# Routed experts: half of the gate weights' row blocks as plain float32, w1 and w3 side by side, no low halves on GpSimd, one path for all block sizes

## The chip, the cores and the metric

The kernel runs on one core of a Trainium2 chip, in one launch. The metric is the device time of one execution in microseconds. A time that is given here is that of the profiled execution, or the median of runs where it says so.

## What is computed

A token sequence of 512 rows and 1024 columns goes through two layers of a hybrid mixer (first_block), then through a layer with differential attention, retention and a mixture of experts. The change lies in the mixture's routed experts alone:

```
_, top_e = lax.top_k(jnp.where(emask, sel, -jnp.inf), TOP_K)      # 8 of 64 experts for each token
...
xb = h_pad[tok]
yb = (jax.nn.silu(xb @ w1[e]) * (xb @ w3[e])) @ w2[e]
return acc.at[tok].add((yb * wt[:, None].astype(yb.dtype)).astype(acc.dtype)), None
```

w1 and w3, the gate weights, are 1024 x 256, w2 is 256 x 1024, all float32: 3 MB for an expert, 64 experts.

## The kernel before

Every operation goes through a recorder (`Rec`, line 411 issues them all, so that the profile shows one line for everything). A planner (`plan`, `attempt`) sorts the recorded operations for each engine by its own costs; the order of the program is its result, and each engine then works in that order. Tiles come from pools: `s2` has 70 half tiles of 128x512 (named b in the profile), `ad` has four whole tiles of 128x1024 (named raw), `wr` three more.

The expert stage (`moe`, line 2280) runs the 64 experts in a fixed order of slots: experts 0 to 3 in the first four, the others sorted by their load when it is known. Each slot has a capacity (`CAPS`: 192, 128, 96, 80, 64, 48 or 32 rows). A slot of 192 is worked in two blocks, of 128 and 64 rows, so there are 68 blocks: 35 of more than 64 rows and 33 of up to 64. A loop behind them takes what did not fit; it is a few instructions if nothing is left.

For an expert:

- `w_raws` (line 2158) loads the weights on the SP queue: twelve half tiles of 128x512, the first two as one whole tile from `ad` (`RAWN`), in the order w1, w3, w2. A load is held back until an earlier expert has reached a certain point (`hold`, `RAHEAD`).
- `w_load` (line 2180) splits each half tile into a high and a low half: ScalarE copies it to the rounded type float32r (hi), and a subtraction raw - hi gives lo. The subtraction is VectorE's (DVE), but for the half tiles 2, 5, 8 and 11 it is GpSimd's (POOL):

```
nc.scalar.activation(hi, raw, AF.Copy)
sub = nc.gpsimd if 4 * i + q in POOL_LO else nc.vector
sub.tensor_tensor(out=lo, in0=raw, in1=hi.bitcast(F32), op=OP.subtract)
```

- `block` (line 2203) makes the list of tokens, gathers their rows X with an indirect DMA of POOL (raw<-h2d), transposes X on TensorE (PE) in two halves of four column blocks, and splits each half into hi and lo.
- `ffn` (line 2109) is the gate pass, the activation and the second product. For a block of more than 64 rows each of 8 column blocks takes three rounded matmuls (hi·hi, hi·lo, lo·hi) for w1 and three for w3, each with 256 moving columns: 48. For a smaller block of c rows hi and lo of X stand side by side as 2c stationary columns, and each column block takes two matmuls for w1 and two for w3: 32; the two parts are then transposed and added (the fold). The second product takes 12 rounded matmuls with 512 columns.
- Y, scaled by the token's weight (two multiplications on DVE, raw<-ps,m,b), stands in a whole tile of the pool `ad` and is added to the result in DRAM by an indirect DMA of POOL (accd<-raw), the scatter.

Of the kernel before, what the change touches and what calls it, by code (L numbers as in the profile page):

```python
# [12 lines left out]
F32 = mybir.dt.float32  # L13
# [21 lines left out]
POOL_LO = (2, 5, 8, 11)  # L35
# [13 lines left out]
FOLD = "v"  # L49
# [93 lines left out]
def layout2(a, o):  # L143
# [20 lines left out]
    for n in ("exp_w1", "exp_w3", "exp_w2"):  # L164
        o[n] = a[n + "_2"][0]
# [1695 lines left out]
class K3(K2):  # L1861
# [247 lines left out]
    def ffn(self, w13, w2, xs, c=128):  # L2109
        nc = self.nc  # L2110
        ph = self.psum("mm")
        for i in range(2):
            self.seen.setdefault(3 * self.turn + i, len(nc.ops))
            po = slice(256 * i, 256 * i + 256)
            if c > 64:
                self.mm3(ph[:c, po], [(xs[k], w13[i][k]) for k in range(8)])
                continue
            for k in range(8):
                for n, w in enumerate(w13[i][k]):
                    nc.tensor.matmul(ph[:2 * c, po], xs[k], w, start=(k + n == 0), stop=(k + n == 8))  # L2120
        th, ac, ha = (self.t2() for _ in range(3))
        pt = self.psum("tr")
        if c > 64:
            th, ac, ha = th[:c, :256], ac[:c, :256], ha[:c, :256]
            a, b = ph[:c, 0:256], ph[:c, 256:512]
        else:
            both, s = self.t2()[:2 * c], self.t2()[:, :4 * c]
            nc.scalar.activation(both, ph[:2 * c], AF.Copy)
            for q in range(4):
                self.tr(pt[:, 2 * c * q:2 * c * q + 2 * c], both[:, 128 * q:128 * q + 128])  # L2130
            parts = pt[:, :8 * c].rearrange("p (q h c) -> p q h c", q=4, h=2)
            s3 = s.rearrange("p (q c) -> p q c", q=4)
            if FOLD == "r":
                nc.vector.tensor_reduce(s3, parts.rearrange("p q h c -> p q c h"), axis=AX.X, op=OP.add)
            else:
                nc.scalar.activation(s3, parts[:, :, 1, :], AF.Copy)
                (nc.vector if FOLD == "v" else nc.gpsimd).tensor_tensor(out=s3, in0=s3, in1=parts[:, :, 0, :], op=OP.add)
            th, ac, ha = th[:, :2 * c], ac[:, :2 * c], ha[:, :2 * c]
            a, b = s[:, :2 * c], s[:, 2 * c:4 * c]
# [3 lines left out]
        if c > 64:  # L2143
            for j in range(2):
                self.tr(pt[:, c * j:c * j + c], ha[:, 128 * j:128 * j + 128])
            ha = pt[:, :2 * c]
        hh, hl = self.t2(F32R, tag="wh")[:, :2 * c], self.t2(F32R, tag="wl")[:, :2 * c]
        nc.scalar.activation(hh, ha, AF.Copy, scale=0.5)
        nc.vector.scalar_tensor_tensor(hl, ha, 0.5, hh.bitcast(F32), op0=OP.mult, op1=OP.subtract)
# [8 lines left out]
    def w_raws(self, es):  # L2158
        nc, A = self.nc, self.A
        for at, e in enumerate(es):  # L2160
            for i, n in enumerate(("exp_w1", "exp_w3", "exp_w2")):
                for h in range(2):
                    big = 2 * i + h in RAWN[min(at, len(RAWN) - 1)]
                    for cs in (slice(0, 1024),) if big else (slice(0, 512), slice(512, 1024)):
                        nc.bias = -STEP * (at + 1)
                        self.hold(3 * at + i - RAHEAD)
                        if i == h == cs.start == 0 and not isinstance(e, int):
                            e = nc.call("sync", *e)
                        f = lambda a, h=h, i=i, cs=cs: (a.rearrange("(h p k) f -> p h (k f)", h=2, k=4) if i < 2 else
                                                        a.rearrange("(j p) d -> p j d", j=2))[:, h, cs]  # L2170
                        raw = self.t2(tag="ad" if big else "s2")
                        if isinstance(e, int):
# [215 lines left out]
```

## Time and profile before

| | us |
|---|---|
| three runs | 2492.75, 2490.65, 2480.94 |
| median | 2490.65 |
| span of the profiled execution (its own time; none is listed apart from it) | 2496.7 |
| PE busy | 2153.1 (86%) |
| DVE busy | 1899.5 (76%) |
| ScalarE busy | 1244.2 (50%) |
| POOL busy | 909.6 (36%) |

The profile is of one execution. Busy times are unions of an engine's instructions over the whole span, so they mix stages with different limits; a stage is read from the slices and from a table by stretches. The last chain of the profile holds only the final few microseconds, and tells nothing of the stage. The expert stage begins at about 1600 us and ends at about 2475 us.

### The profile page before, as it was taken

Reading aid. Unit: us, or ns where it says so; the run is one execution under the profiler, and the core shown is the slowest. Engines: PE = TensorE matmul, PEld = TensorE weight load, DVE = VectorE, ACT = ScalarE, POOL = GpSimd, SP = SyncE. Lnnn points to the kernel's source line nnn. Section 1 sums busy time; section 2 is a strip of 40 time slices with the busy share of each in tenths; the row PEclk is TensorE's granted clock in tenths of the full one; section 3 lists DMA queues with packets and bytes.
Section 4 is the critical chain, followed back from the end, with each engine's and each line's share of the span. In section 5 each row is a group of like instructions: output and inputs, shape, how many; then the busy total and the mean of one; then the engine's idle time right before and its main releaser. Section 6 shows DMA issues by size and latency. Waiting matters only on the chain. (4 is left out here: it accounts for less than half of the span.)

```text
span 2496.7 us, 36786 instructions
## 1 busy us (share of the span) xinstructions
PE 2153.1 (86%) x11824; PEld 1740.9 (70%) x11824; DVE 1899.5 (76%) x3679; ACT 1244.2 (50%) x2594; POOL 909.6 (36%) x649
## 2 busy tenths in 40 slices
PE   6889988999999999999987898778878887777774
PEld 4678865677879877778865686677767766556553
DVE  7994568765885467778426766899999989999996
ACT  6554456443542554544323543455555556566664
POOL 3363334000130000010001221565666777767764
PEclk9998999999999999999989799889999988878987
DMA  5334354223331322241111253688988998888983
GB/s 183 114 104 146 110 167 153 71 64 133 97 96 43 127 80 73 63 158 67 59 43 34 68 194 132 184 262 256 292 260 245 287 276 273 263 267 281 294 259 108
DMA packets 191206, 398.40 MB, mean 160 GB/s; under 512 B 32169, under 2 KB 48297, under 8 KB 191010
## 3 DMA queue, kind: packets, MB, share of 16 engines
q1 hardware_dynamic: 178050, 356.24, 43.2%
q0 software_dynamic: 12960, 39.79, 7.5%
q8 instruction: 93, 1.52, 0.3%
q14 instruction: 103, 0.84, 0.1%
HBM read 358.44 MB, written 41.63 MB: 160 GB/s over the span
## 5 line engine op out<-in xcount | busy, mean ns | idle before, releaser
L411 PE MATMUL ps<-b,b 128*128 128x512 f32 (+11 forms) x9700 | 1956.0, 360 | 187.7 <-DVE b L411 126.5
L411 PEld LDWEIGHTS ps<-b,b 128*128 128x128 f32 (+3 forms) x9700 | 1532.1, 188 | 529.7 <-DVE b L411 156.0
L411 DVE TENSOR_TENSOR b<-b,b 128x512 fp32r<-128x512 f32 (+11 forms) x656 | 574.5, 900 | 34.5 <-ACT b L411 16.7
L411 ACT ACTIVATE b<-b 128x512 fp32r<-128x512 f32 (+6 forms) x896 | 481.3, 594 | 196.3 <-DVE b L411 152.9
L411 ACT ACTIVATE b<-ps 128x512 f32<-128x512 f32 (+13 forms) x661 | 279.1, 445 | 560.3 <-PE ps L411 498.9
L411 DVE TENSOR_TENSOR b<-raw,b 128x512 fp32r<-128x512 f32 (+2 forms) x468 | 379.7, 826 | 186.1 <-ACT b L411 171.6
L411 POOL TENSOR_TENSOR b<-b,b 128x512 fp32r<-128x512 f32 (+2 forms) x318 | 442.6, 1447 | 207.3 <-DVE b L411 99.2
L411 ACT ACTIVATE b<-raw 128x512 fp32r<-128x512 f32 (+3 forms) x476 | 284.7, 614 | 342.5 <-PE ps L411 247.7
L411 PE MATMUL ps<-const,b 128*128 128x128 f32 (+3 forms) x964 | 172.4, 299 | 90.1 <-DVE b L411 71.5
L411 PEld LDWEIGHTS ps<-const,b 128*128 128x128 f32 (+3 forms) x964 | 125.3, 157 | 125.8 <-DVE b L411 80.2
L411 POOL TENSOR_TENSOR raw<-raw,raw 128x1024 f32<-128x1024 f32 x56 | 139.8, 2504 | 156.9 <-ACT raw L411 128.0
L411 POOL TENSOR_TENSOR m<-m,mhalf 128x1 f32<-128x1 f32 (+2 forms) x54 | 53.6, 994 | 302.8 <-DVE m L411 298.5
L411 POOL DMA_INDIRECT raw<-h2d,m x68 | 101.8, 1498 | 167.0 <-DVE m L411 87.2
L411 POOL MEMSET b<- 64x512 f32 (+4 forms) x19 | 8.4, 453 | 399.2 <-PE ps L411 324.6
L411 POOL DMA_INDIRECT accd<-raw,m x72 | 125.2, 1739 | 62.6 <-DVE raw L411 24.3
L411 DVE TENSOR_TENSOR b<-ps,b 128x512 fp32r<-128x512 f32 (+8 forms) x204 | 101.3, 513 | 25.4 <-ACT b L411 16.3
L411 DVE TENSOR_TENSOR b<-b,ps 128x512 f32<-128x512 f32 (+5 forms) x150 | 80.5, 545 | 48.3 <-PE ps L411 46.8
L411 DVE TENSOR_REDUCE m<-ps 128x1 f32<-128x256 f32 (+9 forms) x196 | 74.9, 392 | 41.8 <-PE ps L411 39.9
L411 DVE SCALAR_TENSOR_TENSOR raw<-ps,m,b 96x512 f32<-96x512 f32 (+5 forms) x136 | 95.7, 735 | 6.8 <-PE ps L411 6.8
L411 DVE SCALAR_TENSOR_TENSOR b<-b,b 128x512 f32<-128x512 f32 (+4 forms) x124 | 83.8, 677 | 16.1 <-ACT b L411 11.7
L411 DVE SCALAR_TENSOR_TENSOR b<-ps,cols,b 128x511 f32<-128x511 f32 (+3 forms) x118 | 86.8, 742 | 7.6 <-ACT b L411 6.6
L411 PE MATMUL ps<-const,raw 64*128 64x64 f32 (+5 forms) x544 | 63.5, 257 | 30.6 <-DVE b L411 17.4
(137 smaller groups left out, 1129.4 us busy)
## 6 DMA issues: line engine op xcount, KB each, us to landing
b<-in_exp_w_dram SPq DMA_DIRECT2D x640, 256.0 KB
raw<-in_wi_dram SPq DMA_DIRECT2D x100, 512.0 KB
raw<-in_exp_w_dram SPq DMA_DIRECT2D x64, 512.0 KB
raw<-in_adaw_dram SPq DMA_DIRECT2D x48, 512.0 KB
raw<-in_wo_dram SPq DMA_DIRECT2D x40, 512.0 KB
raw<-in_wuq_dram SPq DMA_DIRECT2D x24, 192.0 KB
b<-in_x_dram SPq DMA_DIRECT2D x16, 256.0 KB
zd<-b SPq DMA_DIRECT2D x16, 256.0 KB
```

Source lines behind the costliest of these rows:

```text
L411: getattr(getattr(nc, o.eng), o.fn)(*[real(x) for x in o.a], **{m: real(x) for m, x in o.k.items()})
```

## The change

The weights of an expert come in one array `ew`: four tiles of 128x1024 for w1 and w3, then two for w2. In a tile of the first four the half tiles are two row blocks k, each with w1's 256 columns and w3's 256 beside each other, so that one matmul with 512 moving columns serves both. Row blocks 0 to 3 (`NATIVE = 4`) are used as they were loaded, with X copied and not split, by one float32 matmul each; row blocks 4 to 7 and w2 are split as before, always with the subtraction on DVE, and take three rounded matmuls each. The path for blocks of up to 64 rows is gone. The whole tile (`RAWN`) now holds row blocks 0 and 1.

```diff
-POOL_LO = (2, 5, 8, 11)
+NATIVE = 4
...
-    for n in ("exp_w1", "exp_w3", "exp_w2"):
-        o[n] = a[n + "_2"][0]
+    w13 = np.stack([a[n + "_2"][0].reshape(64, 2, 128, 2, 2, 256) for n in ("exp_w1", "exp_w3")], axis=5)
+    w2 = a["exp_w2_2"][0].reshape(64, 2, 128, 1024)
+    o["ew"] = np.concatenate([w13.transpose(0, 1, 3, 2, 4, 5, 6).reshape(64, 4, 128, 1024), w2], axis=1)
...
     def ffn(self, w13, w2, xs, c=128):
...
-            if c > 64:
-                self.mm3(ph[:c, po], [(xs[k], w13[i][k]) for k in range(8)])
+        for k in range(8):
...
+            if k < NATIVE:
+                nc.tensor.matmul(ph, xs[k], w13[k], start=(k == 0), stop=(k == 7))
                 continue
-            for k in range(8):
-                for n, w in enumerate(w13[i][k]):
-                    nc.tensor.matmul(ph[:2 * c, po], xs[k], w, start=(k + n == 0), stop=(k + n == 8))
+            (xh, xl), (wh, wl) = xs[k], w13[k]
+            for n, (x, w) in enumerate(((xh, wh), (xl, wh), (xh, wl))):
+                nc.tensor.matmul(ph, x, w, start=(k + n == 0), stop=(k + n == 9))
...
     def w_load(self, at):
...
+            if q < NATIVE:
+                W.append(self.raw[p])
+                continue
...
-                nc.scalar.activation(hi, raw, AF.Copy)
-                sub = nc.gpsimd if 4 * i + q in POOL_LO else nc.vector
-                sub.tensor_tensor(out=lo, in0=raw, in1=hi.bitcast(F32), op=OP.subtract)
+            self.split(self.raw[p], hi, lo)
...
     def block(self, w, pos, aux, c=128):
...
-            if c > 64:
-                hi, lo = self.t2(F32R, tag="wh")[:, :4 * c], self.t2(F32R, tag="wl")[:, :4 * c]
-                self.split(px, hi, lo)
-                xs += [(hi[:, c * k:c * k + c], lo[:, c * k:c * k + c]) for k in range(4)]
+            if h < NATIVE // 4:
+                x = self.t2(tag="wh")[:, :4 * c]
+                nc.scalar.activation(x, px, AF.Copy)
+                xs += [x[:, c * k:c * k + c] for k in range(4)]
                 continue
```

The planner sorts the changed program anew, so the order on every engine is another one from the expert stage on. Three places follow.

POOL in the middle of the stage, before (a gather is raw<-h2d, a scatter accd<-raw; the others are low halves, b<-raw weights and their hi):

```order
L411 DMA raw_150<-h2d,m_17_93 80x1024
L411 TENSOR_TENSOR b_18769<-b_18387,b_18753 128x512
L411 TENSOR_TENSOR b_18802<-b_18434,b_18783 128x512
L411 TENSOR_TENSOR b_18817<-b_18440,b_18806 128x512
L411 DMA accd<-raw_145,m_3_79 640x1024
L411 TENSOR_TENSOR b_18868<-b_18470,b_18843 128x512
L411 DMA raw_151<-h2d,m_50_126 80x1024
L411 TENSOR_TENSOR b_18950<-b_18589,b_18932 128x512
L411 TENSOR_TENSOR b_18963<-b_18593,b_18953 128x512
L411 TENSOR_TENSOR b_18985<-b_18577,b_18973 128x512
L411 TENSOR_TENSOR b_19030<-b_18659,b_19018 128x512
L411 DMA accd<-raw_146,m_1_77 640x1024
```

and now:

```order
L411 DMA raw_150<-h2d,m_28_104 48x1024
L411 DMA accd<-raw_148,m_47_123 640x1024
L411 DMA raw_151<-h2d,m_10_86 48x1024
L411 DMA accd<-raw_145,m_29_105 640x1024
L411 DMA accd<-raw_145,m_8_84 640x1024
L411 DMA raw_149<-h2d,m_9_85 48x1024
L411 DMA raw_150<-h2d,m_5_81 48x1024
```

Between a gather and a scatter nothing is left on POOL.

PE at the head of the gate pass of a block of 64 rows, before (ps is the sum, then X's tile of hi and lo beside each other is the second name, a half of a weight's half tile the first):

```order
L411 MATMUL ps_68<-b_20081,b_20231 128x256
L411 MATMUL ps_68<-b_20106,b_20231 128x256
...
L411 MATMUL ps_68<-b_20114,b_20231 128x256
L411 MATMUL ps_68<-b_20139,b_20231 128x256
...
L411 MATMUL ps_68<-b_20097,b_20239 128x256
L411 MATMUL ps_68<-b_20116,b_20239 128x256
```

and now (raw_147, b_17447 and b_17450 are raw weights, x2 are two in a row):

```order
L411 MATMUL ps_66<-raw_147,b_17815 64x512 x2
L411 MATMUL ps_66<-b_17447,b_17815 64x512
L411 MATMUL ps_66<-b_17450,b_17815 64x512
L411 MATMUL ps_66<-b_17723,b_17828 64x512
L411 MATMUL ps_66<-b_17723,b_17837 64x512
L411 MATMUL ps_66<-b_17738,b_17828 64x512
L411 MATMUL ps_66<-b_17735,b_17828 64x512
L411 MATMUL ps_66<-b_17735,b_17837 64x512
L411 MATMUL ps_66<-b_17744,b_17828 64x512
```

Four matmuls with raw weights and 512 columns stand ahead of the twelve with split ones.

DVE around the writing of two Ys one after the other, with what each instruction waits for (DMASW is a landing of a DMA of POOL's, DMAHW one of SP's), before:

```order
L411 TENSOR_TENSOR b_18992<-b_18582,b_18981 128x512 [waits DMAHW6_49,DVE_49,Activation_49]
L411 SCALAR_TENSOR_TENSOR raw_148<-ps_66,m_12_88,b_11997 80x512 [waits DMASW6_49,DVE_49,PE_49]
L411 SCALAR_TENSOR_TENSOR raw_148<-ps_65,m_12_88,b_12001 80x512 [waits DVE_49,PE_49]
L411 TENSOR_TENSOR b_19038<-b_18655,b_19003 128x512 [waits DMAHW3_49,Activation_49]
...
L411 TENSOR_SCALAR m_39_115<-m_14_90,dumprow 80x1
L411 TENSOR_TENSOR b_19157<-b_18789,b_19145 128x512 [waits DMAHW3_49,Activation_49]
L411 SCALAR_TENSOR_TENSOR raw_147<-ps_66,m_36_112,b_11997 80x512 [waits DVE_49,PE_49]
L411 TENSOR_TENSOR b_19171<-b_18793,b_19161 128x512 [waits DMAHW5_49,Activation_49]
L411 SCALAR_TENSOR_TENSOR raw_147<-ps_65,m_36_112,b_12001 80x512 [waits DVE_49,PE_49]
```

and now:

```order
L411 TENSOR_TENSOR b_17124<-b_16852,b_17113 128x512 [waits DMAHW7_49,Activation_49]
L411 SCALAR_TENSOR_TENSOR raw_146<-ps_66,m_22_98,b_11990 80x512 [waits DMASW1_49,PE_49]
L411 SCALAR_TENSOR_TENSOR raw_146<-ps_65,m_22_98,b_11999 80x512 [waits PE_49]
L411 TENSOR_TENSOR b_17133<-b_16854,b_17120 128x512 [waits DMAHW0_49,Activation_49]
...
L411 TENSOR_TENSOR b_17249<-b_16976,b_17238 128x512 [waits DMAHW1_49,Activation_49]
L411 TENSOR_TENSOR b_17254<-b_16978,b_17245 128x512 [waits DMAHW2_49,Activation_49]
L411 SCALAR_TENSOR_TENSOR raw_146<-ps_66,m_36_112,b_11990 80x512 [waits DMASW3_49,PE_49]
L411 SCALAR_TENSOR_TENSOR raw_146<-ps_65,m_36_112,b_11999 80x512 [waits PE_49]
L411 TENSOR_TENSOR b_17277<-b_17014,b_17261 128x512 [waits DMAHW4_49,Activation_49]
```

The later Y of the changed order goes into the same tile raw_146 as the one before it and waits for a scatter (DMASW3); before, the two Ys stand in raw_148 and raw_147. With it, the whole tile of raw weights waits for PE where it waited for DVE or a scatter, in most of its loads.

## Rows read from the trace of the kernel before

**Rows 1.** The page's 40 equal slices, busy tenths of DVE and DMA.

```profile
DVE  7994568765885467778426766899999989999996
DMA  5334354223331322241111253688988998888983
```

**Rows 2.** Busy us by stretch; columns: length, five engines, granted clock, DMA share, GB/s.

```profile
0.00:1350.00 1350.00, 1249.37 (x6204) 1003.57 (x6205) 898.00 (x1911) 625.11 (x1237) 248.34 (x199) 0.96 0.32 101
...
1570.00:1650.00 80.00, 58.97 (x383) 50.63 (x382) 71.04 (x125) 37.98 (x79) 53.00 (x37) 0.83 0.82 233
1650.00:2050.00 400.00, 333.51 (x2242) 291.10 (x2241) 371.41 (x557) 220.34 (x457) 256.26 (x168) 0.91 0.89 268
1950.00:2050.00 100.00, 86.64 (x591) 73.32 (x590) 89.73 (x143) 57.98 (x122) 70.62 (x43) 0.89 0.91 277
2050.00:2450.00 400.00, 302.13 (x1902) 232.48 (x1901) 373.74 (x615) 249.35 (x547) 287.15 (x187) 0.85 0.84 266
```

**Rows 3.** Waits of 1650 to 2450 us: total, times, longest us.

```profile
PE ps L411 <- DVE b L411: 115.8, 57, 5.5
```

**Rows 4.** Groups of DVE, 1650 to 2450 us; after the bar busy us, mean ns, idle before.

```profile
L411 DVE TENSOR_TENSOR b<-b,b 128x512 fp32r<-128x512 f32 x348 | 381.0, 1125 | 12.0 <-ACT b L411 9.7 <-POOL b L411 1.1 <-issue 0.7
L411 DVE TENSOR_TENSOR b<-raw,b 128x512 fp32r<-128x512 f32 x117 | 123.1, 1068 | 0.2 <-ACT b L411 0.2
L411 DVE SCALAR_TENSOR_TENSOR raw<-ps,m,b 48x512 f32<-48x512 f32 x28 | 19.5, 732 | 0.0
L411 DVE TENSOR_TENSOR b<-ps,b 128x512 fp32r<-128x512 f32 x16 | 10.4, 683 | 3.4 <-ACT b L411 3.3
```

**Rows 5.** Groups of POOL and ScalarE (ACT), 1650 to 2450 us.

```profile
L411 POOL TENSOR_TENSOR b<-b,b 128x512 fp32r<-128x512 f32 x232 | 360.7, 1618 | 59.3 <-ACT b L411 38.4 <-issue 9.1 <-PE ps L411 6.4
L411 POOL DMA_INDIRECT accd<-raw,m x61 | 106.9, 1753 | 41.7 <-DVE raw L411 18.2 <-DVE b L411 10.4 <-issue 7.7
L411 POOL DMA_INDIRECT raw<-h2d,m x61 | 91.8, 1504 | 157.1 <-DVE m L411 81.3 <-DMA b<-in_exp_w_dram 42.1 <-PE ps L411 13.8
...
L411 ACT ACTIVATE b<-b 128x512 fp32r<-128x512 f32 x579 | 317.0, 620 | 5.3 <-DVE b L411 2.7 <-POOL b L411 2.6
```

**Rows 6.** Timeline of DVE, then of POOL, 1692 to 1700 us: start, length.

```profile
1692.22 0.69 DVE L411 TENSOR_TENSOR b<-raw,b 128x512 fp32r<-128x512 f32 x1
1692.83 6.03 DVE L411 TENSOR_TENSOR b<-b,b 128x512 fp32r<-128x512 f32 x1
1698.78 0.68 DVE L411 TENSOR_TENSOR b<-raw,b 128x512 fp32r<-128x512 f32 x1
...
1691.98 1.25 POOL L411 DMA_INDIRECT raw<-h2d,m  x1 [6.29 <-DVE m L411]
1693.26 5.04 POOL L411 TENSOR_TENSOR b<-b,b 128x512 fp32r<-128x512 f32 x4
```

**Rows 7.** Timeline of PE, the two records of one plain float32 matmul.

```profile
263.98 0.59 PE L411 MATMUL ps<-raw,ones 128*1 128x512 f32 x1
...
264.40 0.59 PE L411 MATMUL ps<-raw,ones 128*1 128x512 f32 x1
```

**Rows 8.** Timeline of PE, rounded matmuls with 512 and with 256 columns.

```profile
31.62 2.52 PE L411 MATMUL ps<-b,b 128*128 128x512 f32 x10
...
1971.41 2.27 PE L411 MATMUL ps<-b,b 128*128 128x256 f32 x17
```

**Rows 9.** Stretches of those matmuls, columns as in rows 2.

```profile
263.90:264.90 1.00, 1.00 (x4) 0.09 (x3) 1.00 (x1) 1.00 (x2) 0.91 (x1) 1.00 0.01 4
...
31.60:34.10 2.50, 2.50 (x13) 1.80 (x11) 2.50 (x5) 2.38 (x4) 2.24 (x1) 1.00 0.81 234
...
1971.40:1973.50 2.10, 2.10 (x22) 2.10 (x20) 2.10 (x4) 0.38 (x1) 1.95 (x2) 1.00 1.04 389
```

**Rows 10.** DMA traffic of 1650 to 2450 us.

```profile
DMA packets 101003, 213.26 MB, mean 267 GB/s; under 512 B 12747, under 2 KB 12747, under 8 KB 100920
```

**Rows 11.** The last chain, 2470 to 2480 us: start, length.

```profile
2475.01 3.50 DMA accd<-raw,m
```

More of the change, by code (lines that the diff above doesn't have):

```diff
@@ L48 @@
 YTAG = "ad"
-FOLD = "v"
 HCTAG = "s2"
@@ L2160, in w_raws @@
         for at, e in enumerate(es):
[L2161 to L2172, printed above, removed]
-                            nc.sync.dma_start(raw, f(A[n][e]))
-                        else:
-                            nc.sync.dma_start(raw, Late(lambda r, f=f, n=n: f(A[n][bass.ds(r, 1)].rearrange("a b c -> (a b) c")), e))
-                        yield raw[:, 0:512]
-                        if big:
-                            yield raw[:, 512:1024]
+            for q in range(6):
+                big = q in RAWN[min(at, len(RAWN) - 1)]
+                for cs in (slice(0, 1024),) if big else (slice(0, 512), slice(512, 1024)):
+                    nc.bias = -STEP * (at + 1)
+                    self.hold(3 * at + q // 2 - RAHEAD)
+                    if q == cs.start == 0 and not isinstance(e, int):
+                        e = nc.call("sync", *e)
+                    raw = self.t2(tag="ad" if big else "s2")
+                    if isinstance(e, int):
+                        nc.sync.dma_start(raw, A["ew"][e, q][:, cs])
+                    else:
+                        nc.sync.dma_start(raw, Late(lambda r, q=q, cs=cs: A["ew"][bass.ds(r, 1), q].rearrange("a b c -> (a b) c")[:, cs], e))
+                    yield raw[:, 0:512]
+                    if big:
+                        yield raw[:, 512:1024]
     def w_load(self, at):
@@ L2182, in w_load @@
         W = []
-        for i in range(3):
-            for q in range(4):
-                p = 12 * at + 4 * i + q
-                while self.raws is not None and len(self.raw) <= p + LOOK:
-                    r = next(self.raws, None)
-                    if r is None:
-                        self.raws = None
-                    else:
-                        self.raw.append(r)
-                nc.bias = -STEP * (at + 1)
-                self.hold(3 * at + i - AHEAD)
-                raw, hi, lo = self.raw[p], self.t2(F32R), self.t2(F32R)
-                nc.scalar.activation(hi, raw, AF.Copy)
-                sub = nc.gpsimd if 4 * i + q in POOL_LO else nc.vector
-                sub.tensor_tensor(out=lo, in0=raw, in1=hi.bitcast(F32), op=OP.subtract)
-                W.append((hi, lo))
-        sl = lambda w, o, c: (w[0][:, o:o + c], w[1][:, o:o + c])
-        w13 = [[sl(W[4 * i + k // 2], 256 * (k % 2), 256) for k in range(8)] for i in range(2)]
-        return w13, lambda j, n: W[8 + 2 * j + n]
+        for q in range(12):
+            p = 12 * at + q
+            while self.raws is not None and len(self.raw) <= p + LOOK:
+                r = next(self.raws, None)
+                if r is None:
+                    self.raws = None
+                else:
+                    self.raw.append(r)
+            if q < NATIVE:
+                W.append(self.raw[p])
+                continue
+            nc.bias = -STEP * (at + 1)
+            self.hold(3 * at + q // 4 - AHEAD)
+            hi, lo = self.t2(F32R), self.t2(F32R)
+            self.split(self.raw[p], hi, lo)
+            W.append((hi, lo))
+        return W[:8], lambda j, n: W[8 + 2 * j + n]
     def block(self, w, pos, aux, c=128):
```

44 lines of the change are left out of this document (12 added, 32 removed).

## The prediction, made before the changed kernel ran

> **What bounds the kernel now.** I read the slices first. From slice 25 on, VectorE (DVE) stands at 8 or 9 tenths and the DMA engines too [rows 1]; this is the expert stage. The table by stretches makes it exact. From 1650 to 2450 us DVE is busy 371.4 + 373.7 = 745 of 800 us, TensorE (PE) 333.5 + 302.1 = 636, GpSimd (POOL) 543, and the DMA share averages 0.865, which is 692 us of full work [rows 2]. Sixty-one of the 68 blocks lie in it (the first three and the last four don't), and about 58 experts' weights. Then I asked who waits: of PE's 164 idle us, 116 end with a DVE result [rows 3]. So DVE is the bound here, with DMA and PE close behind.
>
> Why is DVE so busy? Its costliest group is the subtraction that makes a low half, 348 + 117 = 465 of them, on average 1125 and 1068 ns; the same shape with one operand in PSUM takes 683 [rows 4]. The timeline tells the reason: one such subtraction lasts 6.03 us from 1692.83, and in that time POOL runs four of its own, one behind the other, for 5.04 us from 1693.26. The one before it began 0.61 us earlier, and the next one starts when POOL has ended [rows 6]. A DVE subtraction with both operands in SBUF stands still while POOL does the same kind of work. Four low halves of each expert are POOL's, 232 in the stretch at 1618 ns [rows 5].
>
> **The change, part by part.**
> *Low halves on POOL go.* The 232 instructions (360.7 us of POOL, [rows 5]) disappear. Four of an expert's twelve half tiles are no longer split; the eight that are left are all split on DVE, as many as before. At 0.61 us each [rows 6] the 465 subtractions would fill 284 us; they fill 381.0 + 123.1 = 504 [rows 4]. The gain on DVE is 220 us. POOL keeps 61 gathers and 61 scatters (91.8 + 106.9 us, [rows 5]). I take no standstill from these: the subtraction at 1692.22 ran wholly beside a gather and took 0.69 us [rows 6]. If they held DVE as subtractions do, 220 x 199/361 = 121 us of the excess would stay; that is the other end.
> *One split of X per block goes.* The first four column blocks of X get one copy on ScalarE only. DVE saves at most 0.68 us a block [rows 4], some 0.4 at a mean width of about 75 rows: 24 us. DVE after: 745 - 220 - 24 = 501 us.
> *The small path goes.* A block of up to 64 rows loses a copy, a fold and two of four transposes, and its gate instructions run on c rows of 256 columns instead of 128 rows of 2c. On ScalarE and DVE this is about even, and the slack above hides it; I cost it at nothing. Without that slack it could cost or give a few tenths of a us a block. ScalarE also loses 4 x 58 copies of 0.62 us [rows 5], 144 us off the path.
> *PE.* A plain float32 matmul with 512 columns leaves two records, 0.42 us apart (263.98 and 264.40, [rows 7]) at a granted clock of 1.00 [rows 9]; I take 0.86 us for one. Ten rounded ones of that width take 2.52 us, or 0.23 each without the tail of the last; with 256 columns seventeen take 2.27, or 0.12 each [rows 8], both at 1.00 [rows 9]. A gate pass after the change is 4 x 0.86 + 12 x 0.23 = 6.2 us. Before it was 48 x 0.12 = 5.76 us for a block over 64 rows (32 in the stretch) and 32 x 0.12 = 3.84 for a small one (29). So PE gains 32 x 0.44 + 29 x 2.36 = 82 us of work at full clock, 94 at the stretch's mean clock of 0.88 [rows 2]: 636 + 94 = 730 us busy.
> *DMA.* The new array holds the same bytes in the same 65 whole and 650 half tiles, the loop's included, and a half row is still 2 KB. The 692 us [rows 2] stay.
> *Waits that are added or moved.* The order shows that nearly every Y now uses the tile of the Y before, so a Y waits for the last scatter: 1.75 us of issue [rows 5] and 3.50 to land [rows 11], 5.25 us. Besides Y's two multiplications of 0.73 us [rows 4], DVE has 501/61 - 1.5 = 6.7 us of work a block, which hides it; uncovered, it would hold every split that stands behind Y. The whole tile of raw weights is now freed by PE, after its second plain matmul, and not by the split; three tiles go round, so the load that waits there is some three experts ahead of PE. Plain operands wait for their load directly, with no split between.
>
> What is late next? DVE, with 501 us, is out of the way. Two resources are left.
> DMA has 692 us of work, and its best 100 us stretch reached a share of 0.91 [rows 2]. At 0.91 the stretch takes 760 us, at 0.96 it takes 721, at 1.00 it takes 692.
> PE has 730 us at today's clock. In the first 1350 us, which have little POOL work, it was busy 1249.4/1350 = 0.925 at clock 0.96 [rows 2]. At that share and today's clock: 730/0.925 = 789 us; with the clock at 0.96: 730 x 0.88/0.96/0.925 = 723.
> I take 750, a little under the middle of PE's two (756), since the clock is higher where PE is busier (0.85, 0.91, 0.96 in the three long rows, [rows 2]); it lies within the DMA bounds too. That is 50 us less, and 5 us more for the seven blocks outside the stretch, where DVE shows 71 of 80 us [rows 2]. Sum: -55 us.
> On DMA the Trainium skill differs: DMA: Bandwidth & Descriptors, Specifications, puts the limit of one core at about 358 GB/s. By it the stretch's 213.26 MB [rows 10] would be an estimated 596 us, DMA no bound, and the sum PE's own, 756 us and thus 49 less all told. No stretch of 400 us here passed 268 GB/s though its engines were 0.89 busy, so I keep the row.
>
> The profiled execution spans 2496.7 us, 6 us or 0.24% above the median of the three runs (2490.65). Taken off the median: about **2435 us**, 2.2% faster. What a measurement can tell from no change is about 0.5%, or 12 us.
>
> **The rivals.**
> *DMA runs full and PE keeps up.* The new order has far fewer loads that wait for a tile, and then 692 us decide, 108 less: about 2383. Against it: no 100 us was over 0.91 [rows 2].
> *PE is the bound and its clock stays.* 789 us, -11 and -5: about 2475. For it: 0.85 in the late experts, with PE 76% busy. Against it: the clock in the busier stretches [rows 2].
> *DVE's relief buys nothing.* If a share of 0.865 is all that the engines give in this mix of loads, gathers and scatters, the stretch stays at 800 us: about 2490. The same would come if the edit did not free DVE because gathers and scatters held it. For it: the DMA digits, 8 and 9 in nearly every late slice [rows 1]. Against it: slices of 8 and of 9 alternate, and most of PE's idle time ends with DVE, not with a load [rows 3]. The Trainium skill leans this way: SBUF — State Buffer, A bandwidth-pool intuition that's wrong, says that HBM is almost always the bottleneck from end to end.
> *Slower: PE goes cold.* PE has more to do, and its weights come straight from loads that are near their own limit. If it stands still for a load before gate passes and finds itself at the lower clock behind each such gap, the passes stretch. With the idle time that does not end with DVE today (164 - 116 = 48 us) the stretch is 730 x 0.88/c + 48 at a mean clock c; at 0.80 that is 851, 51 more: about 2540. It decides from c = 0.854 downwards, where 800 us are reached. For it: 0.83 from 1570 to 1650 and 0.85 at the end [rows 2]. Against it: the gaps that DVE made go.
>
> **How the numbers follow.** Forecast, a stretch of 720 to 775 us (2405 to 2460): 0.53. Full DMA (below 2405): 0.10. PE at its old clock (2460 to 2478): 0.15. Nothing gained (2478 to 2503): 0.08. Cold PE (over 2503): 0.14. Faster by over 0.5% are the first three, 0.78; within it 0.08; slower 0.14. The range 2380 to 2500 leaves out some 0.05 below it, and above it the slower rival, 0.14.
>
> **What would show it.** Right: hardly a DVE subtraction of the stage over 0.75 us and their mean near 0.68; DVE near 0.67 of the stage and POOL under 0.3; the plain matmuls as pairs of records 0.43 us apart; PE over 0.9 busy and DMA over 0.9, with PE's waits ended by loads or ScalarE. Wrong: DVE still over 0.9 (then it was not POOL's subtractions); or DVE free and the stage as long, at a DMA share of 0.87 (loads were the bound) or at a clock under 0.85 (cold PE); or long waits of DVE for a scatter in front of Y.

## The result, and the profile of the changed kernel

The changed kernel takes 2392.56 us (median of 4 runs, 2384.61 to 2396.73) against 2491.7 for the kernel before in the same comparison: a ratio of 0.9603, 95% interval 0.9576 to 0.9631. The forecast was 2435 in a range of 2380 to 2500. The direction and the range held; the gain was 99 us where 55 were forecast.

The profiled span went from 2496.7 to 2395.0 us. The page of the changed kernel: busy time, and three of its rows of slices (40 slices, tenths).

```profile
span 2395.0 us, 32613 instructions
PE 2187.3 (91%) x10382; PEld 1546.5 (65%) x10382; DVE 1619.6 (68%) x3578; ACT 1087.7 (45%) x2272; POOL 534.6 (22%) x393
...
DVE  7995577775695557767733675657676667776775
...
PEclk9998999899999999999998979989999999999998
DMA  5334354223222232314211025349999899999994
```

From slice 28 on (1617 us) DVE stands at 6 and 7 where it stood at 8 and 9, and the DMA engines stand at 9 nearly throughout where 8 and 9 alternated [rows 1]; the last slice of each kernel holds the end of the stage. The table by stretches (length, the five engines, granted clock, DMA share, GB/s) shows where the 100 us went:

```profile
0.00:1350.00 1350.00, 1250.78 (x6220) 1005.64 (x6221) 899.77 (x1926) 627.20 (x1243) 250.96 (x205) 0.96 0.32 101
1570.00:1650.00 80.00, 66.96 (x275) 42.28 (x275) 47.76 (x115) 31.57 (x64) 35.38 (x23) 0.85 0.71 206
1650.00:2000.00 350.00, 326.10 (x1384) 192.20 (x1384) 241.29 (x507) 155.75 (x329) 104.96 (x59) 0.95 0.95 297
2000.00:2350.00 350.00, 335.02 (x1433) 150.84 (x1432) 252.90 (x563) 168.54 (x375) 97.45 (x62) 0.97 0.97 316
```

The first 1350 us are what they were [rows 2]. The expert stage from 1650 us on, which took 800 us, takes 700: what is left behind it is 45 us, as before (46.7). In those 700 us PE is busy 661 (0.945) at clock 0.96, the DMA share is 0.96 (672 us of full work), DVE is busy 494 (0.71) and POOL 202 (0.29). Before, over 800 us: PE 636 at 0.88, DMA 0.865, DVE 745, POOL 543 [rows 2]. The traffic of the stage is that of before [rows 10], in less time:

```profile
DMA packets 101720, 214.51 MB, mean 306 GB/s; under 512 B 12767, under 2 KB 12767, under 8 KB 101657
```

The groups behind that (after the bar: busy us, mean ns, idle before), 1650 to 2350 us, first DVE, then POOL:

```profile
L411 DVE TENSOR_TENSOR b<-b,b 128x512 fp32r<-128x512 f32 x459 | 290.1, 682 | 8.0 <-ACT b L411 5.3 <-issue 0.6 <-DMA raw<-in_ew_dram 0.4
...
L411 POOL DMA_INDIRECT accd<-raw,m x62 | 116.1, 1873 | 329.7 <-DVE raw L411 199.8 <-DVE m L411 63.2 <-DVE b L411 55.4
L411 POOL DMA_INDIRECT raw<-h2d,m x59 | 86.6, 1467 | 172.6 <-PE ps L411 80.8 <-issue 56.5 <-DMA accd<-raw,m 18.1
```

459 subtractions of 682 ns stand where 465 of 1125 and 1068 stood [rows 4]; POOL's 232 are gone, a gather lasts about as long as before (1467 ns against 1504) and a scatter a little longer (1873 against 1753) [rows 5]. The waits of the same stretch (total us, times, longest us), of PE, DVE and of SP's own queue:

```profile
PE ps L411 <- DMA raw<-h2d,m: 26.3, 13, 4.7
...
PE ps L411 <- DVE b L411: 1.8, 2, 1.1
...
DVE raw L411 <- DMA accd<-raw,m: 25.2, 12, 5.3
...
SPq L411 <- PE ps L411: 133.7, 73, 14.1
```

PE's wait for a DVE result in a half tile (b), 115.8 us before [rows 3], is 1.8. Most of what is left of PE's 39 us of idle time ends with gathers of X. The plain matmuls stand in PE's timeline (start, length) as forecast; four records, which are two plain matmuls, take 1.92 us with the tail of the last, or some 0.44 a record without it (the tail is 0.59 - 0.42 = 0.17 us by [rows 7]):

```profile
2204.10 1.92 PE L411 MATMUL ps<-raw,b 128*48 128x512 f32 x4
```

### The profile page after: what moved, and what is told of

Read it like the earlier page. It is cut to its first block, busy times and chain, and to the rows that moved or that the text cites. A ratio compares the mean times of both kernels' runs of the same rounds, so it can differ in the third digit from the quotient of the medians.

```text
span 2395.0 us, 32613 instructions
## 1 busy us (share of the span) xinstructions
PE 2187.3 (91%) x10382; PEld 1546.5 (65%) x10382; DVE 1619.6 (68%) x3578; ACT 1087.7 (45%) x2272; POOL 534.6 (22%) x393
## 4 chain that ended last, share of the span: by engine, by line
PE 69%; DVE 13%; DMA 11%; ACT 3%; issue 3%; POOL 1%; SPq 0%; POOLq 0%; DVEq 0%; ACTq 0%
PE ps L411 69%; DVE b L411 10%; DMA raw<-h2d,m 5%; DVE m L411 3%; ACT b L411 3%; DMA accd<-raw,m 1%; DMA raw<-in_adaw_dram 1%; DMA raw<-in_wo_dram 1%; DMA b<-in_ew_dram 1%; POOL raw L411 1%; DMA xdiag<-b 0%; DMA raw<-in_wi_dram 0%; SPq L411 0%; DMA raw<-accd 0%; DMA b<-in_x_dram 0%
## 5 line engine op out<-in xcount | busy, mean ns | idle before, releaser
L411 PE MATMUL ps<-b,b 128*128 128x512 f32 (+9 forms) x8052 | 1870.1, 389 | 83.2 <-DVE b L411 49.6
L411 PEld LDWEIGHTS ps<-b,b 128*128 128x128 f32 (+6 forms) x8052 | 1312.6, 184 | 571.9 <-issue 130.1
L411 ACT ACTIVATE b<-ps 128x512 f32<-128x512 f32 (+16 forms) x661 | 271.1, 431 | 676.6 <-PE ps L411 599.6
L411 DVE TENSOR_TENSOR b<-b,b 128x512 fp32r<-128x512 f32 (+5 forms) x751 | 469.8, 664 | 35.2 <-ACT b L411 18.3
L411 ACT ACTIVATE b<-b 128x512 fp32r<-128x512 f32 (+3 forms) x702 | 393.8, 619 | 121.6 <-DVE b L411 84.5
L411 DVE TENSOR_TENSOR b<-raw,b 128x512 fp32r<-128x512 f32 (+2 forms) x340 | 240.0, 720 | 187.2 <-ACT b L411 173.7
L411 PE MATMUL ps<-const,b 128*128 128x128 f32 (+5 forms) x898 | 159.5, 292 | 52.1 <-DVE b L411 39.0
L411 PEld LDWEIGHTS ps<-const,b 128*128 128x128 f32 (+5 forms) x898 | 115.0, 153 | 102.0 <-DVE b L411 49.4
L411 PE MATMUL ps<-raw,b 128*96 128x512 f32 (+5 forms) x272 | 151.8, 676 | 5.3 <-ACT raw L411 2.9
L411 DVE SCALAR_TENSOR_TENSOR raw<-ps,m,b 96x512 f32<-96x512 f32 (+5 forms) x136 | 97.5, 740 | 50.9 <-DMA accd<-raw,m 30.1
L411 DVE TENSOR_TENSOR b<-b,ps 128x512 f32<-128x512 f32 (+6 forms) x150 | 82.6, 559 | 49.2 <-PE ps L411 48.5
```

What stands on the lines that cost most here:

```text
L411: getattr(getattr(nc, o.eng), o.fn)(*[real(x) for x in o.a], **{m: real(x) for m, x in o.k.items()})
```

## The experiments

Three questions were open. Was it the end of POOL's subtractions that freed DVE? Which of the change's parts are needed? And what bounds the stage now, PE or the transfers? The table gives each kernel's median, its ratio to the kernel before with its interval, and the difference to the changed kernel, worked out as the difference of the ratios times 2491.7 us.

| kernel | us | ratio, 95% interval | against the changed kernel |
|---|---|---|---|
| changed kernel | 2392.6 | 0.9603 (0.9576 to 0.9631) | |
| changed + 4 POOL subtractions (a_pool) | 2522.6 | 1.0116 (1.0083 to 1.0148) | +128 |
| before, all subtractions on DVE (b_pool0) | 2519.8 | 1.0105 (1.0059 to 1.0152) | +125 |
| before, small path off (b_one) | 2505.9 | 1.0046 (1.0023 to 1.0069) | +110 |
| before, both (b_one_pool0) | 2430.5 | 0.9739 (0.9698 to 0.9780) | +34 |
| changed, no plain row blocks (n0) | 2420.8 | 0.9714 (0.9679 to 0.9749) | +28 |
| changed, 2 plain (n2) | 2396.6 | 0.9618 (0.9568 to 0.9667) | +4 |
| changed, all 8 plain (n8) | 2465.5 | 0.9891 (0.9858 to 0.9924) | +72 |
| changed, one product less (a_pe) | 2365.9 | 0.9513 (0.9473 to 0.9553) | -22 |
| changed, 0.5 MB less (a_dma) | 2407.1 | 0.9687 (0.9640 to 0.9734) | +21 |
| both cuts (a_both) | 2336.4 | 0.9390 (0.9345 to 0.9435) | -53 |
| one product less, order kept (s_pe) | 2370.6 | 0.9517 (0.9490 to 0.9544) | -21 |
| 0.2 MB more, order kept (x_dma) | 2414.2 | 0.9711 (0.9677 to 0.9745) | +27 |

### GpSimd's subtractions put back: a_pool

```diff
             if q < NATIVE:
                 W.append(self.raw[p])
+                nc.bias = -STEP * (at + 1)
+                self.hold(3 * at + q // 4 - AHEAD)
+                nc.gpsimd.tensor_tensor(out=self.t2(F32R), in0=self.raw[p], in1=self.g2[0], op=OP.subtract)
                 continue
```

> The changed kernel with the suspected cost put back and nothing else: for each of an expert's four plain half tiles GpSimd subtracts a constant row tile from the raw weights into a tile that nobody reads, 256 subtractions of 128x512. The output is unchanged. Theory (they hold VectorE): VectorE gets some 220 us of standstill on top of 508 in the stretch of 700 us, over its end: 728/0.95 = 766 us, about 2460 us in all (2435 to 2485), and VectorE's subtractions last up to some 6 us again. Rival (VectorE now has slack enough, or GpSimd is harmless): within 10 us of 2392.6.

Measured: 2522.6 us. DVE's and POOL's groups, 1650 to 2450 us:

```profile
L411 DVE TENSOR_TENSOR b<-b,b 128x512 fp32r<-128x512 f32 x448 | 467.7, 1092 | 5.8 <-ACT b L411 3.5 <-DMA b<-in_ew_dram 0.2
...
L411 POOL TENSOR_TENSOR b<-raw,b 128x512 fp32r<-128x512 f32 x114 | 164.8, 1487 | 0.9
L411 POOL TENSOR_TENSOR b<-b,b 128x512 fp32r<-128x512 f32 x112 | 144.9, 1332 | 0.7
```

Four subtractions per expert whose result nobody reads bring the mean of DVE's back from 682 to 1092 ns and take the whole gain away. The standstill is POOL's doing: 226 POOL subtractions of 310 us cost DVE 448 x 0.41 = 184 us. Counted over this stretch of the trace, the 364 DVE subtractions that overlap none of POOL's last 676 ns on average and 745 at most, and the 81 that overlap one last 2975 on average. The price in time is larger than the theory's, above its 2435 to 2485 us, and was not traced further: DVE is busy 682 of the 800 us, PE 687, and the DMA share is 0.87, so no one of them is full.

### The same step alone, in the kernel before: b_pool0

```diff
-POOL_LO = (2, 5, 8, 11)
+POOL_LO = ()
```

> The kernel before with one number changed: all twelve low halves of an expert are subtracted on VectorE, none on GpSimd. Theory (GpSimd's subtractions hold VectorE's): VectorE loses 220 us of standstill and gains 232 x 0.61 = 142 us of work in the stretch of 61 blocks, 745 to 667 us; loads (692 us of work) and VectorE then end close together and the stretch takes about 715 instead of 800 us, so about 2405 us in all (2385 to 2430). Rival (GpSimd's help was worth its price, and the gain of the change comes from the splits that it leaves out): VectorE, the bound, gets half as many subtractions again, 745 + 142 = 887 us, and the kernel is slower, towards 2570; at the least it is no faster than 2485.

Measured: 2519.8, slower by 1%. The theory's 2385 to 2430 was missed. The time lies where the rival put it (no faster than 2485), but not for the rival's reason, a DVE with 887 us of work: DVE is busy 625 of the 800 us. DVE's groups (1650 to 2450 us) show that the standstill is gone; the stretches show that the stage does not profit:

```profile
L411 DVE TENSOR_TENSOR b<-b,b 128x512 fp32r<-128x512 f32 x554 | 357.5, 679 | 0.0
L411 DVE TENSOR_TENSOR b<-raw,b 128x512 fp32r<-128x512 f32 x110 | 73.1, 678 | 0.0
```

```profile
1650.00:2050.00 400.00, 341.27 (x2354) 293.85 (x2354) 337.68 (x702) 231.21 (x481) 159.68 (x64) 0.92 0.92 282
2050.00:2450.00 400.00, 288.16 (x1641) 210.56 (x1639) 287.40 (x647) 217.79 (x482) 149.16 (x55) 0.82 0.78 241
```

In the second half, where the small blocks are, every resource has room: PE 0.72 at clock 0.82, DVE 0.72, DMA 0.78. A new wait stands there (1650 to 2450 us):

```profile
POOL accd L411 <- DVE raw L411: 216.8, 44, 14.2
PEld ps L411 <- DMA raw<-h2d,m: 127.4, 37, 9.6
PE ps L411 <- DMA raw<-h2d,m: 115.7, 34, 9.4
```

PE waits 116 us for gathers, as long as it had waited for DVE [rows 3]. My reading is that the gathers are late because a scatter stands ahead of them in POOL's queue that waits for its Y, and because they need a row index that comes from PE, through DVE, behind the block before (POOL's timeline in the last section shows one whose wait of 10.69 us PE ended). In POOL's order in the traces the middle one of the 68 gathers has two scatters more ahead of it than in the kernel before. No run changes that place alone.

### The small path off, alone and together: b_one, b_one_pool0

```diff
-            if c > 64:
+            if c > 0:
```

(at the four places of the diff; in b_one_pool0 with `POOL_LO = ()` too)

> The kernel before with the special path for small blocks off alone (blocks of 64 rows or fewer take the path of the large ones); the GpSimd subtractions and the split of all gate weights stay. TensorE gets the rounded matmuls of a large block for 29 small ones, 29 x 1.92 = 56 us, in a stretch (2050 to 2450 us) where it was busy for 302 of 400. Theory, VectorE is what bounds the kernel before, through the subtractions that stand still beside GpSimd's, and the small path's copies, transposes and sum lie beside other work: 2480 to 2510, no change that can be told. Rival, the small path's longer way from the gate product to the second product costs by itself: 2420 to 2470. Rival, TensorE's added 56 us count: 2530 or more.

Measured: 2505.9, no gain and half a per cent slower; the theory's range held. DVE's subtractions still stand still (1650 to 2350 us):

```profile
L411 DVE TENSOR_TENSOR b<-b,b 128x512 fp32r<-128x512 f32 x298 | 329.9, 1139 | 6.7 <-ACT b L411 5.1 <-DMA b<-in_exp_w_dram 0.7 <-issue 0.7
```

> The kernel before with the small path off and all subtractions on VectorE. It does the work of the changed kernel without plain row blocks and without the gate weights side by side. With the subtractions on VectorE alone the time did not fall (2520), and its trace had TensorE waiting for gathers in the half with the small blocks; in GpSimd's order there each gather stands behind two scatters more than in the kernel before, here as well. Theory, the small path's longer way to Y holds the scatters, and the gathers behind them, so the gain of the lock's end shows only once that path is gone too: 2410 to 2435, like the changed kernel without plain row blocks (2421). Rival, the gathers' place behind the scatters is the cause by itself: 2500 to 2530. Rival, the gate weights side by side (one 512-column matmul in place of two of 256) carry the rest: 2450 to 2490.

Measured: 2430.5, as the theory said. Neither part gains by itself (1.0105 and 1.0046); if they simply added up, both would give 1.015. They give 0.974, so 4.1%, or 103 us, come from having both. The stretches and PE's wait of b_one_pool0 (the wait from 1650 to 2350 us):

```profile
1650.00:2050.00 400.00, 348.66 (x2420) 300.96 (x2419) 338.24 (x700) 227.79 (x474) 143.86 (x64) 0.93 0.94 285
2050.00:2450.00 400.00, 322.77 (x2237) 241.21 (x2235) 327.57 (x709) 224.98 (x490) 201.07 (x65) 0.92 0.81 255
```

```profile
PE ps L411 <- DMA raw<-h2d,m: 44.4, 24, 5.8
```

The gathers stand as far behind the scatters as in b_pool0 (the middle one again has two more ahead of it than in the kernel before), so their place alone is not the cause: with the longer way from the gate product to Y gone, and with more PE work per small block, PE's wait for them falls to 44 us and its clock in the second half is 0.92 instead of 0.82. Which of these two does it, the shorter way or the added work, was not separated.

The gate weights side by side show no effect that can be told: 0.9739 here, 0.9714 in n0, which has them.

### How many row blocks plain: n0, n8, n2

```diff
-NATIVE = 4
+NATIVE = 0
```

> The changed kernel with no plain matmul at all (NATIVE = 0): all eight row blocks are split on VectorE and take three rounded matmuls with 512 columns each; one path for all sizes, w1 and w3 side by side, nothing but gathers and scatters on GpSimd. A gate pass on TensorE is 24 x 0.23 = 5.5 us instead of 6.2, VectorE has 501 + 142 + 24 = 667 us of work in the stretch of 61 blocks. Theory (GpSimd's subtractions were the cost, the plain matmuls are not what made it faster): about 2400 us (2385 to 2425), within 1% of the changed kernel's 2392.6. Rival (the splits that plain matmuls save are what made it faster): more than half of the gain of 99 us is lost, over 2445.

> The changed kernel with all eight row blocks of the gate weights plain (NATIVE = 8): VectorE has only w2's four splits of an expert left, a gate pass on TensorE is 8 x 0.86 = 6.9 us instead of 6.2. Theory (TensorE is a bound of the changed stage, 661 of 700 us busy): 61 x 0.7 = 43 us more work at full clock, at a busy share of 0.945 and clock 0.96 about 46 us more in the stretch and 50 in all, about 2440 us (2425 to 2455). Rival (loads are the bound, DMA share 0.96, and TensorE has room): within 10 us of 2392.6.

> The changed kernel with the gate weights' row blocks 0 and 1 plain in place of 0 to 3; blocks 2 and 3 are split like the rest. Per block TensorE does 2 x (0.86 - 3 x 0.23) = 0.34 us less, 21 us over 61 blocks; VectorE and ScalarE get two more splits per expert (2 x 0.68 and 2 x 0.62 us, 83 us of VectorE over 61, to 577 of 700) and the split of half of X's first half. Theory, TensorE and the transfers bound the stage together: TensorE's 21 us come off an engine that the transfers hold anyway, and VectorE's added work is covered for the most part: 2385 to 2405. Rival, TensorE alone: 2370 to 2380. Rival, VectorE's work counts wherever it is added, as the run without plain blocks suggests (28 us for four more splits): 2403 to 2412.

Measured: 2420.8 with none, 2396.6 with 2, 2392.6 with 4, 2465.5 with 8. (For n2 the block's code was widened to copy half of the first half of X and split the other half.) None and 2 lie in the ranges of their theories, though none is 1.2% off the changed kernel and not within 1%; 8 lies above its own, 2425 to 2455. Each of these kernels is planned anew, so its order differs as well as its work. Stretches of n0, then of n8:

```profile
1650.00:2000.00 350.00, 310.99 (x1469) 215.23 (x1468) 299.81 (x620) 206.55 (x428) 105.95 (x58) 0.93 0.94 289
2000.00:2350.00 350.00, 317.72 (x1484) 168.41 (x1482) 315.15 (x683) 219.87 (x473) 183.21 (x59) 0.93 0.94 299
```

```profile
1650.00:2050.00 400.00, 360.30 (x1299) 180.89 (x1297) 166.61 (x384) 104.28 (x231) 95.06 (x62) 0.94 0.89 273
2050.00:2400.00 350.00, 334.70 (x1269) 131.54 (x1268) 161.10 (x391) 96.77 (x239) 86.79 (x61) 0.99 0.97 308
```

Without plain blocks DVE is at 615 of 700 us (0.88) and PE at 629; with eight DVE falls to 328 of 750 and the time rises, since each plain row block of the weights adds 0.86 - 3 x 0.23 = 0.17 us of PE per block of tokens, 4 x 0.17 x 61 = 41 us at full clock and 43 at 0.96. The other 29 us or so of n8's 72 go beyond that and were not traced to one cause. In the profiled runs the stretch is 50 us longer (750 against 700); PE is busy 34 us more in it (695 against 661) and idle 16 us more, and its waits for gathers are 50.9 us against 26.3. Two and four are not told apart. So most of the gain, 0.0286 of 0.0397, needs no plain matmul at all; four plain blocks add the last 28 us.

### PE or the transfers: a_pe, a_dma, a_both

```diff
-            for n, (x, w) in enumerate(((xh, wh), (xl, wh), (xh, wl))):
-                nc.tensor.matmul(ph, x, w, start=(k + n == 0), stop=(k + n == 9))
+            for n, (x, w) in enumerate(((xh, wh), (xl, wh))):
+                nc.tensor.matmul(ph, x, w, start=(k + n == 0), stop=(k + n == 8))
```

```diff
+                    if q == 5:
+                        yield kept[cs.start // 512]
+                        continue
                     raw = self.t2(tag="ad" if big else "s2")
...
+                    if q == 4:
+                        kept = [raw[:, 0:512]] if cs.start == 0 else kept + [raw[:, 0:512]]
                     yield raw[:, 0:512]
```

> The changed kernel with the third of the three rounded products (high part of X by low part of the gate weights) left out for row blocks 4 to 7: that part of the gate product is not computed. It takes 4 x 0.23 = 0.92 us of TensorE time from each block, 56 us over the 61 or so blocks of the expert stage (1650 to 2350 us), where TensorE was busy for 661 of 700 us and the DMA engines for 0.96 of the time. Theory, TensorE and the transfers bound the stage together (672 us of DMA work at 214.5 MB lie under the 700): the transfers keep the stage at 690 or so, 2375 to 2392 in all, and the granted clock falls below 0.96. Rival, TensorE alone sets the pace: the stage loses nearly the whole 56 us, 2335 to 2350. Rival, neither of them but the chain between engines: within 5 us of the changed kernel, with the DMA share unchanged.

> The changed kernel with the second half of each expert's third weight matrix not loaded (the tiles of its first half are used again): the last product is computed with the wrong rows, so it leaves 0.5 MB of 3.5 MB of traffic per block out, 32 MB in the expert stage, some 100 us of DMA work at 306 GB/s. TensorE's work is the same. Theory, TensorE and the transfers bound the stage together (661 and 672 us of work under 700): TensorE now goes on alone, 665 to 680 us for the stage, 2360 to 2375 in all, with TensorE busy for over 0.97 and a DMA share of 0.85 or less. Rival, the transfers alone set the pace: the stage loses 60 us or more (TensorE's clock would have to rise above 0.96), below 2340. Rival, TensorE alone sets it: within 5 us of the changed kernel.

> Both of the cuts at once: the third rounded product of row blocks 4 to 7 left out, and the second half of the third weight matrix not loaded. TensorE has some 605 us of work in the expert stage at the clock of the changed kernel, the transfers 575, VectorE 494. Theory, TensorE and the transfers bound the stage together: each cut alone is held by the other, both together give more than the sum of the two alone, 620 to 650 us for the stage, 2315 to 2345 in all. Rival, one of the two alone sets the pace: both together give no more than the better of the two alone. Rival, the chain between engines: 2370 or above.

Measured: -22, +21 and -53 us against the changed kernel. a_pe (2365.9) lies between the ranges of its theory and of its rival, a_both where the theory put it. The cut of PE's work gives less than half of its 56 us; the cut of traffic gives nothing and costs some; both together give nearly all of PE's 56. Stretches of a_dma:

```profile
1650.00:2000.00 350.00, 331.32 (x1438) 197.08 (x1437) 251.46 (x533) 161.49 (x344) 126.12 (x63) 0.98 0.89 267
2000.00:2350.00 350.00, 322.84 (x1350) 146.43 (x1348) 237.03 (x526) 158.01 (x351) 106.11 (x59) 0.94 0.83 255
```

With the DMA share down to 0.86, PE is still busy 654 of 700 us, about as before: this speaks against the transfers holding PE in the changed kernel. But a_dma missed all three expectations, since none allowed for a loss. Its instructions come in another order, as the planner sees fewer loads; that this costs the 21 us was not shown. The next two runs therefore change nothing in the order.

### The same two questions with every queue's order kept: s_pe, x_dma

```diff
         for o in order:
+            if getattr(o, "skip", False):
+                continue
...
                 nc.tensor.matmul(ph, x, w, start=(k + n == 0), stop=(k + n == 9))
+                nc.ops[-1].skip = n == 1
```

```diff
                 getattr(getattr(nc, o.eng), o.fn)(*[real(x) for x in o.a], **{m: real(x) for m, x in o.k.items()})
+                if getattr(o, "skip", False):
+                    at = 64 * (self.dup % 2)
+                    self.dup += 1
+                    nc.sync.dma_start(self.scr[at:at + 64], real(o.a[1])[at:at + 64, 0:384])
...
+                    nc.ops[-1].skip = q == 5
                     yield raw[:, 0:512]
```

> The changed kernel with one of the three rounded products (low part of X by high part of the gate weights) not issued for row blocks 4 to 7, so that this part of the gate product is not computed. Unlike the earlier cut of the other product, these instructions are dropped behind the planner, so every engine's order stays that of the changed kernel, only shorter by 4 x 0.23 = 0.92 us of TensorE time per block, 56 us in the stage. Theory, the transfers stand right behind TensorE: the stage comes down to their 672 us of work and no further, 2360 to 2375 in all, as with the other order (2366). Rival, TensorE alone sets the pace and the earlier cut was spoilt by its order: 2335 to 2350. Rival, the order is what gave the earlier gain: 2380 or above.

> The changed kernel with 0.2 MB of traffic per expert added behind the planner: behind each of the two loads of the third matrix's second half, 64 of its 128 rows of 1.5 KB are loaded once more into a tile that nobody reads. Every engine's order stays that of the changed kernel; 12 MB more in the stage, 39 us of DMA work at 306 GB/s, to some 710 where the stage takes 700. Theory, TensorE and the transfers bound the stage together: the added work shows for the most part, 2412 to 2432. Rival, TensorE alone sets the pace and the transfers still have room: within 8 us of the changed kernel, up to 2400.

Measured: 2370.6 and 2414.2, both where the theory put them. Stretches of s_pe, then of x_dma:

```profile
1650.00:2000.00 350.00, 316.35 (x1322) 180.53 (x1321) 251.05 (x528) 164.55 (x348) 109.95 (x62) 0.95 0.99 312
2000.00:2325.00 325.00, 293.50 (x1225) 126.38 (x1225) 236.69 (x531) 158.09 (x352) 94.66 (x59) 0.95 0.98 320
```

```profile
1650.00:2000.00 350.00, 323.29 (x1359) 190.41 (x1357) 237.35 (x499) 154.54 (x326) 101.46 (x58) 0.94 1.02 310
2000.00:2350.00 350.00, 331.11 (x1415) 149.88 (x1413) 251.35 (x555) 171.96 (x367) 98.84 (x62) 0.97 1.03 323
```

With 56 us of PE work gone the stage ends some 25 us earlier, PE is busy 610 of 675 us, and the DMA share is 0.99 and 0.98: the 675 us are filled by transfers. With 39 us of transfers added the share reads 1.02 and 1.03 and 27 of the 39 us show. Over these stretches the two kernels move the same 316 GB/s, where the changed kernel moves 306 (first s_pe, then x_dma):

```profile
DMA packets 101067, 213.15 MB, mean 316 GB/s; under 512 B 12689, under 2 KB 12689, under 8 KB 101006
...
DMA packets 108480, 221.51 MB, mean 316 GB/s; under 512 B 14258, under 2 KB 21326, under 8 KB 108416
```

PE's new idle time in s_pe ends with gathers of X, not with loads of weights. Its wait for them was 26.3 us in the changed kernel:

```profile
PE ps L413 <- DMA raw<-h2d,m: 51.5, 25, 5.3
```

The profile's chain through the changed kernel's stage (1650 to 2350 us, followed back from the last instruction) says the same: 72.7% of it is PE, 15.9% gathers, and 2.7% loads of weights into half tiles. So I read PE as what sets the pace of the changed kernel, with the transfers right behind it: 21 to 25 of 700 us by s_pe, 39 - 27 = 12 by x_dma, each uncertain by some 10 us, and a share of 0.96. Whatever takes more than that from PE meets them. Two things were not separated: whether the gathers of s_pe are late because the engines are full or by their place in POOL's queue, and what a cut of traffic alone would give with the order kept.

The best kernel that does the whole computation is the changed one, with the variant of two plain blocks beside it. a_pe and s_pe are faster, but they leave a product out.

## Why the prediction was right, and where its size was off

**DVE was the bound, by standing still beside POOL.** The standstill is right, and shown both ways: 682 ns without POOL's subtractions, 1092 with four dead ones, 1139 in b_one, where they stay. DVE came out at 494 us where 501 were worked out. That DVE was the bound, so that freeing it is enough, is not borne out: b_pool0 frees it (745 to 625 us) and is no faster.

**Gathers and scatters cost DVE nothing.** Right: 62 + 59 of them are there, and the mean is 682 ns, as in b_pool0 with 679.

**PE's work.** 730 us at clock 0.88 were forecast; at 0.96 that is 730 x 0.88/0.96 = 669, and 661 were measured. So the prices (0.86, 0.23, 0.12) held in sum.

**The step that failed is "I take 750"** for the stretch of 800 us. It lay between PE's two ends, 723 at clock 0.96 and 789 at 0.88; the stretch took 700. Two of its inputs were too low. The clock went to 0.96, the upper of the two that I had taken, in a stage where PE is busy for 0.945, where 0.925 had been taken from the first 1350 us: 661/0.945 = 700. And the DMA engines, which I had seen at 0.91 at best [rows 2], ran at 0.96 over the whole stretch, and moved the same bytes in 672 us of work, 20 less than before. The 5 us for the rest of the program became 1.7. By these the forecast was 50 us short in the stretch and 3 too generous outside it. The rival next to the result was full DMA with PE keeping up (2383); I had held against it that no 100 us was over 0.91, but that row comes from a stretch in which DVE was busy for 0.90 [rows 2], and it bounds no stretch without that.

**The small path costed at nothing.** About right for its removal alone (1.0046, a little slower) and wrong as a step of a sum. POOL's subtractions alone, the edit from which I drew the whole gain, gave no gain in the kernel before (1.0105). Only with the small path gone as well does the time of DVE turn into time of the kernel. The forecast held because the change contains both; that the second part was needed I had not seen, and in this it was lucky.

**The waits that were added.** Right: Y waits for the scatter before it 12 times, 25.2 us in 700, and DVE has 206 us idle; loads that wait for PE to free a tile (SP's 133.7 us) leave the DMA share at 0.96. PE's own waits end with gathers (26.3 us) and ScalarE (5.1), and hardly with loads of weights, which my signs had put first.

**The rivals.** PE at its old clock, nothing gained and cold PE fell: the clock is 0.95 and 0.97 in the two halves. Of the Trainium skill's two rules: the 358 GB/s of DMA: Bandwidth & Descriptors, Specifications, are not reached by any long stretch here, the fastest of 350 us being 323 GB/s at a share that reads 1.03. By that figure the 213.15 MB of s_pe would be an estimated 595 us, no bound, and PE's full 56 us would have been gained; 21 were. The other, SBUF — State Buffer, A bandwidth-pool intuition that's wrong, has HBM as the bottleneck from end to end almost always; here the transfers (no run tells HBM from the engines that move the bytes) come second, right behind PE, in the changed kernel, and first only once PE's work is cut.

**A reading that was off.** Slice 25 shows 6 for DVE and 3 for DMA; the digits 8 and 9 begin at slice 26 for DVE and 27 for DMA [rows 1]. No sum uses it.

## What to carry to other kernels

When a bound is removed, ask of each part of an edit whether it can gain alone: two of these parts lose by themselves and gain 2.6% together, so a sum of separate prices can come out near the total while the part that it names as the cause gains nothing by itself. A stretch with two engines near their limit should be estimated with the share and clock that the engines reach when nothing else holds them, not with the best seen while a third engine held them both. To test a bound in a program whose order is planned, cut or add work behind the planner; a cut ahead of it (a_dma) changes the order too.

## What the runs showed that I had not expected

The standstill seems to work in the other direction as well: POOL's gathers and scatters are drawn out while DVE subtracts. In b_pool0 a gather lasts 7.30 us, and in its first 4.8 us DVE runs one subtraction behind the other with hardly a break. POOL's timeline of b_pool0, then DVE's (start, length):

```profile
2201.98 7.30 POOL L411 DMA_INDIRECT raw<-h2d,m  x1 [1.84 <-issue]
2209.58 1.37 POOL L411 DMA_INDIRECT accd<-raw,m  x1 [0.30 <-issue]
2221.64 1.86 POOL L411 DMA_INDIRECT raw<-h2d,m  x1 [10.69 <-PE ps L411]
```

```profile
2201.99 0.68 DVE L411 TENSOR_TENSOR b<-raw,b 128x512 fp32r<-128x512 f32 x1
2202.59 0.68 DVE L411 TENSOR_TENSOR b<-b,b 128x512 fp32r<-128x512 f32 x1
2203.19 0.24 DVE L411 SCALAR_TENSOR_TENSOR b<-b,b 128x96 f32<-128x96 f32 x1
2203.36 1.45 DVE L411 TENSOR_TENSOR b<-b,b 128x512 fp32r<-128x512 f32 x3
2204.73 0.24 DVE L411 SCALAR_TENSOR_TENSOR b<-b,b 128x96 fp32r<-128x96 f32 x1
2204.90 1.88 DVE L411 TENSOR_TENSOR b<-b,b 128x512 fp32r<-128x512 f32 x3
```

Counted over the 118 gathers and scatters of b_pool0 from 1650 to 2450 us, the time that one lasts, less the time within it in which DVE ran such subtractions of 128x512, is 0.81 us on average and 2.1 at most, though these subtractions fill only 0.56 of the stretch. Eight overlap none of them, and last 1.5 us at most. And in the three kernels that differ in the plain row blocks alone the mean scatter grows with the splits of weights that DVE does per expert: 1788 ns with 4 (n8), 1873 with 8 (the changed kernel, above), 3090 with 12 (n0). The number of splits is not all of it: b_one, with 8 on DVE and another path and order, has 2462. POOL's groups of n8, then of n0, 1650 to 2450 us:

```profile
L411 POOL DMA_INDIRECT accd<-raw,m x66 | 118.0, 1788 | 374.3 <-DVE m L411 187.9 <-DVE raw L411 173.1 <-DVE b L411 10.1
L411 POOL DMA_INDIRECT raw<-h2d,m x61 | 70.7, 1159 | 229.1 <-issue 121.8 <-DMA accd<-raw,m 85.8 <-PE ps L411 14.6
```

```profile
L411 POOL DMA_INDIRECT accd<-raw,m x64 | 197.8, 3090 | 288.4 <-DVE raw L411 188.4 <-DVE b L411 88.5 <-DVE m L411 4.8
L411 POOL DMA_INDIRECT raw<-h2d,m x61 | 119.0, 1951 | 151.7 <-PE ps L411 80.6 <-issue 20.9 <-DVE raw L411 16.0
```

No run isolates this; it is read from the traces. The Trainium skill, SBUF — State Buffer, Who interferes with whom, tells of GpSimd's DMAs starved by VectorE, but infers that a two-input subtraction does not do it; these rows speak against that, as far as rows without a run of their own can. If the reading holds, plain blocks, which spare DVE its splits, also bring the gathers forward, on which PE's last idle time ends.
